# State-space parameters and their powers placed ahead of the modulation's weights, low parts of the first weight columns on VectorE, in a hybrid decoder trunk

## The chip, the cores and the metric

The kernel runs on one core of one Trainium2 chip. A core has five engines with queues of their own: TensorE (PE, with PEld for its weight loads), VectorE (DVE), ScalarE (ACT), GpSimd (POOL) and SyncE (SP), which here only issues DMA transfers. ScalarE's queue issues some transfers too. The metric is the device time of one execution in microseconds; the value for a kernel is the median of its runs.

## The reference

One layer of a trunk, with a prompt of 2048 tokens and 8 short samples of 4 tokens (32 in all), 1024 features, float32. Cut to what matters here:

```python
mod = jnp.dot(jax.nn.silu(c), p['ada_w']) + p['ada_b']
sh1, sc1, g1, sh2, sc2, g2 = jnp.split(mod, 6, axis=-1)
h = x * (1.0 + sc1) + sh1
z = jnp.dot(h, p['in_proj'])            # columns: gate | recurrent | state-space
dt = jnp.exp(log_dt)[:, None]
mag = jnp.exp(dt * ar)
abr, abi = mag * jnp.cos(dt * ai), mag * jnp.sin(dt * ai)
den = ar * ar + ai * ai
nr = abr - 1.0
qr, qi = (nr * ar + abi * ai) / den, (abi * ar - nr * ai) / den
bbr = qr[..., None] * b_re - qi[..., None] * b_im
...
```

A complex diagonal scan with (abr, abi), a gated unit, a real-gated recurrence on the other columns, an output projection, two layer norms and a squared-ReLU MLP follow. The kernel writes the state-space scan in blocks of 8 steps, so that it needs the powers 0 to 8 of abr + i abi.

## The kernel before, in words

Every product is made from a high part (rounded to the fast matmul format) and a low part (the rest): `split` (L77) copies the source to the high part on ScalarE and subtracts it on the engine that it is given. Three matmuls (L373 to L375) make one product.

The opening has this order in the program. ScalarE's queue loads the conditioning vectors c (`crow`), which give `cT`. `ada_early` (L468) loads the weights of modulation section 1, the scale (eight loads of 512 KB on SP's queue), multiplies them with `cT` into `pa`, and between them lets ScalarE's queue issue the 11 loads of small vectors (`vjobs`, L457 to L465: first `ada_b` into `rtA`, then ten into `rtB`). `vec_fin` (L477) transposes them. `ada_fin` (L188) copies `pa` to `adasb`, sums it with `pm` and adds `ada_b` into `mods`; then comes `sc1p`. `load_x` (L385) and `make_h` (L394) bring the first 256 tokens in, transpose them into PSUM (`pt`), scale them into `hf` (VectorE and ScalarE in turns), store `hf` in DRAM (`Hd`) and split it into `a0h` and `a0l`. `load_w` (L197) brings the four column blocks 8 to 11 of in_proj, the state-space columns, into `rwin` and splits them into `hwin` and `lwin`; `WX` (L382) names the engine of each low part: VectorE for the first, GpSimd for the three others. Then `load_x(1)` and `vec_fin("B")`.

After that the generator `s5` (L1457) is made and run to its first yield (L503). This first part loads the state-space parameters with nine small loads on SP's queue (L1513 to L1523; `load`, L1466, puts each behind the last large load), transposes them (`s5pt`), makes dt and mag with two exponentials of some 20 small VectorE operations each (`expf`), sine and cosine on ScalarE, the powers PR and PI (L1555 to L1572), rho, A4r and A4i, then qr, qi and, from the loads of Br and Bi, bbr and bbi (L1580 to L1614), and last copies powers with ScalarE into Q1, Q2, R1, R2 (eight operations of 64x256, L1616 to L1624). Br and Bi stand in the same slots as `rw` and the intermediates of the powers.

`pa0` (L504) brings modulation section 0, the shift, in the same way as section 1. The loop at L514 goes over the eight pieces of 256 tokens: it makes the next piece's h (from piece 2, `BARE`, on with the shift in it), runs `s5` on by one part, multiplies the four column blocks with the piece (`accb`), copies the results (`xb`) and stores them in DRAM (`Ud`). The later parts of `s5` make matrices (Bx, CA, kt) from Q1 to R2, bbr, bbi and the C parameters on VectorE and GpSimd and store them (`BCd`, `Td`). Behind the loop, pairs of state-space groups (`pair`) run between the other columns' products.

The order of each engine's queue is not that of the source. The program is built with `schedule_with_timeline_sim=True` (L1895): at build time, whatever the build holds ready goes to its engine, what stands earlier in the program first, by the build's own picture of durations and landings. On the chip each engine then works its queue in that fixed order, and a head that waits holds all behind it. Tiles with the same tag share a fixed number of buffers.

Of the kernel before, what the change touches and what calls it, by code (L numbers as in the profile page):

```python
# [17 lines left out]
P = 128  # L18
# [17 lines left out]
def trunk(ctx: ExitStack, tc: tile.TileContext, *args):  # L36
# [325 lines left out]
    with lpool("ab") as ab:  # L362
# [19 lines left out]
        WX = V, Q, Q, Q  # L382
# [85 lines left out]
        def ada_early(sec, tile_):  # L468
            pa = ptile([P, 512], "D", f"pa{sec}")
            for k in range(0, KD, 2):  # L470
                ada_mm(pa, k, [ada_load(sec, k + e, tile_(f"ada{sec}_{k + e}")) for e in range(2)])
                for _ in range(2):
                    if vjobs:
                        S.dma_start(*vjobs.pop(0))
            return pa
# [11 lines left out]

        pa1 = ada_early(1, early_tile)
        while vjobs:
# [9 lines left out]
        s5x = ExitStack()  # L499
        s5g = s5(s5x, nc, tc, a, outs, rpool, ptile, ident, (Ud, Yd, BCd, Td), dict(  # L500
            tt=tt, mul=mul, add=add, sub=sub, ts=ts, stt=stt, act=act, f32=f32, split=split, last=last_pair))
# [955 lines left out]
def s5(ctx, nc, tc, a, outs, rpool, ps, ident, scratch, o):  # L1457
# [8 lines left out]
    def load(out, in_):  # L1466
        with tc.issue_after(last[0]):
            SP.dma_start(out, in_)
# [33 lines left out]
    with rpool("s5b") as pool:  # L1502
# [11 lines left out]
        for i, key in enumerate(("s5_a_re", "s5_a_im")):  # L1514
            src = a[key][0]
            load(rw[0:32, i, 0:64], src)
            load(rw[0:32, i, 64:128], src)
            load(rw[32:48, i, :], src.rearrange("(p q) n -> p (q n)", q=2))
        ld2 = one([W, 2], "ld2")
        sl = a["s5_log_dt"]  # L1520
        load(ld2[0:32, 0:1], sl.rearrange("o g -> g o"))
        load(ld2[0:32, 1:2], sl.rearrange("o g -> g o"))
        load(ld2[32:48, :], sl[0].rearrange("(p q) -> p q", q=2))  # L1523
# [55 lines left out]

        nr = small("nr", 32)  # L1580
# [34 lines left out]

        Q1 = one([P, 32, 8], "Q1")  # L1616
        Q2 = one([P, 32, 8], "Q2")
        R1 = one([P, 32, 8], "R1")
        R2 = one([P, 32, 8], "R2")
        for dst, s0, half, sg, src in ((Q1, 7, top, 1, PR), (Q1, 7, bot, 1, PI), (Q2, 7, top, -1, PI),  # L1620
                                       (Q2, 7, bot, 1, PR), (R1, 1, top, 1, PR), (R1, 1, bot, -1, PI),
                                       (R2, 1, top, -1, PI), (R2, 1, bot, -1, PR)):
            x = src[half, 7::-1, GB] if s0 == 7 else src[half, 1:9, GB]
            act(dst[half], x.rearrange("p m g -> p g m"), AF.Copy, scale=float(sg))  # L1624
# [274 lines left out]
```

## Time and profile before

| what | value |
|---|---|
| time, median of 3 runs | 2111.79 us (2110.53 to 2115.14) |
| the profiled execution's own time | 2115.44 us |
| span of its profile | 2113.7 us |
| mean granted TensorE clock | 0.986 |
| busy: PE, DVE, ACT, POOL | 2011.9, 1543.5, 1087.4, 494.0 us |

The profile is of one execution. Busy time is the union of an engine's instructions. A granted clock of 1 means the higher of TensorE's two levels, 2.4 GHz, over the whole stretch; at the lower, 1.2 GHz, it reads 0.5. The DMA share is the mean over 16 DMA engines and can exceed 1 a little, as packets overlap. Small differences between times of one kernel, of a few us, are its spread.

### The profile page before, as it was taken

To read this page: it belongs to the slowest core of one execution; us is meant where nothing else is said; L and a number is where in the kernel's file an instruction comes from. 1 tells how busy PE (TensorE), PEld (TensorE's weight loads), DVE (VectorE), ACT (ScalarE), POOL (GpSimd) and SP (SyncE) were. 2 spreads that over 40 slices of the span, in tenths; PEclk is the share of its full clock that TensorE was granted. 3 is DMA by queue.
4 is the path that set the end of the run, shared out by engine and by line. 5 is a ranking of instruction groups with operands and counts; after the bars stand their busy time and mean duration, and the time that the engine had idled before them with its cause. 6 is when DMAs were issued, how large, how long until landed. Compare 5 with 4: busy or idle time off the path is not lost.

```text
span 2113.7 us, 35579 instructions
## 1 busy us (share of the span) xinstructions
PE 2011.9 (95%) x13055; PEld 1904.1 (90%) x13055; DVE 1543.5 (73%) x2920; ACT 1087.4 (51%) x2077; POOL 494.0 (23%) x327
## 2 busy tenths in 40 slices
PE   7998999889999989999999899999999999999996
PEld 4897888887877879999999899999999999999996
DVE  5678897467887899989898965666747555655587
ACT  3446665445766447554646454635445344444452
POOL 2255333323433233222223300101012001010103
PEclk9999999999999999999999999999999999999998
DMA  9799765543434467968677797878678968686861
GB/s 329 177 263 274 233 197 171 141 137 80 130 94 99 134 244 265 346 248 306 239 278 264 266 323 248 305 268 288 243 260 317 315 229 282 216 270 239 265 218 54
DMA packets 363037, 489.08 MB, mean 231 GB/s; under 512 B 126939, under 2 KB 264575, under 8 KB 362863
## 3 DMA queue, kind: packets, MB, share of 16 engines
q1 hardware_dynamic: 359415, 485.52, 69.6%
q8 instruction: 103, 1.69, 0.3%
q10 hardware_dynamic: 3448, 1.29, 0.2%
q14 instruction: 71, 0.58, 0.1%
HBM read 347.73 MB, written 139.00 MB: 230 GB/s over the span
## 4 chain that ended last, share of the span: by engine, by line
PE 63%; DVE 19%; DMA 6%; issue 5%; ACT 4%; POOL 1%; SPq 1%; ACTq 0%; DVEq 0%; POOLq 0%
PE m1a L1078 19%; PE m2x L1225 13%; PE m1s L1078 8%; PE m2s L1225 6%; PE m2a L1225 3%; DVE xc L62 2%; DVE acc L44 1%; PE accg L373 1%; PE accg L374 1%; PE accg L375 1%; PE op L963 1%; PE pa L185 1%; PE op L964 1%; PE op L962 1%; DVE gi L347 1%
## 5 line engine op out<-in xcount | busy, mean ns | idle before, releaser
L44 POOL TENSOR_TENSOR y<-y,ln_g 128x512 f32<-128x512 f32 (+3 forms) x28 | 36.5, 1320 | 645.8 <-ACT y L65 544.2
L65 ACT ACTIVATE hid<-hid 128x346 f32<-128x346 f32 (+1 forms) x240 | 116.1, 489 | 71.1 <-DVE hid L62 64.3
L65 ACT ACTIVATE ht<-hid 128x692 fp32r<-128x692 f32 (+1 forms) x92 | 72.0, 783 | 127.8 <-PE m2a L1225 38.9
L44 DVE TENSOR_TENSOR lt<-hid,ht 128x692 fp32r<-128x692 f32 (+1 forms) x92 | 85.2, 927 | 40.5 <-ACT ht L65 40.5
L44 DVE TENSOR_TENSOR acc<-m2x,acc 128x346 f32<-128x346 f32 (+1 forms) x168 | 84.1, 511 | 32.0 <-PE m2x L1225 31.7
L44 DVE TENSOR_TENSOR hid<-hid,hid 128x692 f32<-128x692 f32 (+1 forms) x92 | 87.1, 947 | 23.5 <-ACT hid L65 23.3
L1225 PE MATMUL m2x<-ht,hw2s 128*128 128x348 f32 (+1 forms) x352 | 87.7, 322 | 1.8 <-DVE acc L44 1.8
L62 DVE SCALAR_TENSOR_TENSOR hid<-m1s,vecB,u 128x346 f32<-128x346 f32 (+1 forms) x94 | 53.5, 573 | 45.0 <-ACT u L65 35.4
L65 ACT ACTIVATE u<-m1a 128x346 f32<-128x346 f32 (+1 forms) x96 | 43.5, 453 | 70.4 <-PE m1a L1078 63.0
L44 DVE TENSOR_TENSOR lb<-hid,hb 128x692 fp32r<-128x692 f32 (+1 forms) x69 | 69.2, 1004 | 4.7 <-ACT hb L65 4.5
L65 ACT ACTIVATE hb<-hid 128x692 fp32r<-128x692 f32 (+1 forms) x69 | 53.8, 783 | 21.6 <-PE m2a L1225 6.9
L1225 PEld LDWEIGHTS m2x<-ht,hw2s 128*128 128x128 f32 x352 | 61.9, 189 | 2.2 <-ACT hw2s L65 2.1
L65 ACT ACT_TABLE_LOAD x40 | 51.3, 1283 | 15.9 <-DVE hgb L57 6.5
L44 DVE TENSOR_TENSOR acc<-m2s,acc 128x346 f32<-128x346 f32 (+1 forms) x120 | 55.7, 508 | 4.1 <-PE m2s L1225 4.0
L1078 PE MATMUL m1s<-h2t13h,hw1s 128*128 128x348 f32 (+1 forms) x200 | 54.1, 329 | 3.9 <-DVE x L62 3.5
L1225 PE MATMUL m2x<-lt,hw2s 128*128 128x348 f32 (+1 forms) x176 | 56.1, 321 | 0.9 <-DVE lt L44 0.9
L1225 PE MATMUL m2x<-ht,w2s 128*128 128x346 f32 (+1 forms) x216 | 55.9, 321 | 0.0
L1225 PE MATMUL m2s<-ht,hw2s 128*128 128x348 f32 (+1 forms) x208 | 53.2, 331 | 2.6 <-ACT ht L65 2.6
L44 DVE TENSOR_TENSOR u<-m1s,u 128x346 f32<-128x346 f32 (+1 forms) x48 | 24.7, 514 | 42.0 <-PE m1s L1078 27.2
L65 ACT ACTIVATE y<-y,AB,mods 128x128 f32<-128x128 f32 (+2 forms) x96 | 37.5, 472 | 34.5 <-DMA y<-Cd 34.5
L1225 PE MATMUL m2a<-hb,hw2a 128*128 128x348 f32 (+1 forms) x200 | 52.0, 327 | 3.4 <-DVE acc L44 3.4
L1078 PE MATMUL m1a<-h2b1h,hw1a 128*128 128x348 f32 (+1 forms) x208 | 55.1, 323 | 0.0
(854 smaller groups left out, 7982.0 us busy)
## 6 DMA issues: line engine op xcount, KB each, us to landing
W1d<-hw1s SPq DMA_DIRECT2D x53, 512.0 KB
W2d<-hw2s SPq DMA_DIRECT2D x53, 512.0 KB
w1s<-W1d SPq DMA_DIRECT2D x45, 512.0 KB
lw1s<-W1d SPq DMA_DIRECT2D x43, 512.0 KB
hw2s<-W2d SPq DMA_DIRECT2D x41, 512.0 KB
hw1s<-W1d SPq DMA_DIRECT2D x40, 512.0 KB
w2s<-W2d SPq DMA_DIRECT2D x40, 512.0 KB
lw2s<-W2d SPq DMA_DIRECT2D x39, 512.0 KB
```

The source lines that it names most:

```text
L44: return eng.tensor_tensor(out=out, in0=in0, in1=in1, op=op)
L62: return V.scalar_tensor_tensor(out, in0, s, in1, op0, op1)
L65: return S.activation(out, in_, f, **kw).ins
L185: PE.matmul(pa[q:q + 32, :], cT[:, k + e, :], w[:, n * 512:n * 512 + 512], start=(k == 0), stop=(k == KD - 2), tile_position=(0, q))
L347: V.tensor_tensor_scan(gi[:, f, :n], rr[:, f, :n], gi[:, f, :n], 0.0 if pi == 0 else rgs["h"][:, f:f + 1], ALU.mult, ALU.add)
L373: PE.matmul(acc[:, :nt], wh[:, k, :], hh[:, kk, :nt], start=(k == 0), stop=False)
L374: PE.matmul(acc[:, :nt], wh[:, k, :], hl[:, kk, :nt], start=False, stop=False)
L375: PE.matmul(acc[:, :nt], wl[:, k, :], hh[:, kk, :nt], start=False, stop=(k == KD - 1))
L962: PE.matmul(ac[:w, :], yh[:, kk, o:o + w], wh[:, hs], start=(k == 0), stop=False)
L963: PE.matmul(ac[:w, :], yl[:, kk, o:o + w], wh[:, hs], start=False, stop=False)
L1078: PE.matmul(ps, x[:, k, :], h[:, k, o:o + w], start=(on is None and k + i == 0), stop=(k == 3 and i == 2), skip_group_check=on is not None)
L1225: PE.matmul(ps[2 * s_ + jj], x[:, f, js], h[:, f, :], start=(fresh and n + f + e == 0), stop=(n == len(pairs) - 1 and f + e == 3), skip_gr ...
```

## The change

It moves the making of the generator `s5` and its first run ahead of `ada_early(1)`, and gives `s5` one yield more, so that this first run ends behind the powers; the copies into Q1 to R2 now stand ahead of that yield, and the part with qr, qi, Br, Bi, bbr and bbi stays where the whole first part stood. The nine small loads are issued by ScalarE's queue in place of SP's, without the order behind the last large load. The low parts of all four first column blocks are made on VectorE.

```diff
-        WX = V, Q, Q, Q
+        WX = V, V, V, V
...
+        s5x = ExitStack()
+        s5g = s5(s5x, nc, tc, a, outs, rpool, ptile, ident, (Ud, Yd, BCd, Td), dict(
+            tt=tt, mul=mul, add=add, sub=sub, ts=ts, stt=stt, act=act, f32=f32, split=split, last=last_pair))
+        next(s5g)
         pa1 = ada_early(1, early_tile)
         while vjobs:
             S.dma_start(*vjobs.pop(0))
...
         load_x(1)
         vec_fin("B")
-        s5x = ExitStack()
-        s5g = s5(s5x, nc, tc, a, outs, rpool, ptile, ident, (Ud, Yd, BCd, Td), dict(
-            tt=tt, mul=mul, add=add, sub=sub, ts=ts, stt=stt, act=act, f32=f32, split=split, last=last_pair))
 
         next(s5g)
...
-            load(rw[0:32, i, 0:64], src)
-            load(rw[0:32, i, 64:128], src)
-            load(rw[32:48, i, :], src.rearrange("(p q) n -> p (q n)", q=2))
+            S.dma_start(rw[0:32, i, 0:64], src)
+            S.dma_start(rw[0:32, i, 64:128], src)
+            S.dma_start(rw[32:48, i, :], src.rearrange("(p q) n -> p (q n)", q=2))
...
-        load(ld2[0:32, 0:1], sl.rearrange("o g -> g o"))
-        load(ld2[0:32, 1:2], sl.rearrange("o g -> g o"))
-        load(ld2[32:48, :], sl[0].rearrange("(p q) -> p q", q=2))
+        S.dma_start(ld2[0:32, 0:1], sl.rearrange("o g -> g o"))
+        S.dma_start(ld2[0:32, 1:2], sl.rearrange("o g -> g o"))
+        S.dma_start(ld2[32:48, :], sl[0].rearrange("(p q) -> p q", q=2))
...
         V.tensor_copy(A4i[bot], PI[bot, 4, GB])
+
+        Q1 = one([P, 32, 8], "Q1")
+        Q2 = one([P, 32, 8], "Q2")
+        R1 = one([P, 32, 8], "R1")
+        R2 = one([P, 32, 8], "R2")
+        for dst, s0, half, sg, src in ((Q1, 7, top, 1, PR), (Q1, 7, bot, 1, PI), (Q2, 7, top, -1, PI),
+                                       (Q2, 7, bot, 1, PR), (R1, 1, top, 1, PR), (R1, 1, bot, -1, PI),
+                                       (R2, 1, top, -1, PI), (R2, 1, bot, -1, PR)):
+            x = src[half, 7::-1, GB] if s0 == 7 else src[half, 1:9, GB]
+            act(dst[half], x.rearrange("p m g -> p g m"), AF.Copy, scale=float(sg))
+        yield
 
         nr = small("nr", 32)
...
         add(V, bbi, bbi, bt)
-
...
         yield
```

The lines left out ahead of the last yield are the same block of Q1 to R2, taken from there.

## Rows read from the trace of the kernel before

**Rows 1.** The page's parts 1 and 4: busy time, and the chain that ended last.

```profile
PE 2011.9 (95%) x13055; PEld 1904.1 (90%) x13055; DVE 1543.5 (73%) x2920; ACT 1087.4 (51%) x2077; POOL 494.0 (23%) x327
...
PE 63%; DVE 19%; DMA 6%; issue 5%; ACT 4%; POOL 1%; SPq 1%; ACTq 0%; DVEq 0%; POOLq 0%
```

**Rows 2.** Busy time by stretch: PE, PEld, DVE, ACT, POOL, granted clock, DMA share, GB/s.

```profile
21.50:40.00 18.50, 15.37 (x98) 12.91 (x98) 15.36 (x53) 8.06 (x13) 7.76 (x3) 0.91 0.86 296
40.00:64.00 24.00, 24.00 (x165) 17.19 (x165) 19.81 (x125) 8.10 (x17) 2.37 (x1) 1.00 0.65 242
64.00:81.00 17.00, 12.75 (x87) 11.49 (x86) 11.28 (x21) 11.93 (x20) 4.86 (x2) 0.90 0.73 159
81.00:140.00 59.00, 57.82 (x522) 56.00 (x520) 48.09 (x68) 25.82 (x49) 27.27 (x12) 1.00 1.03 262
...
160.00:185.00 25.00, 19.55 (x152) 18.85 (x152) 20.80 (x25) 18.79 (x41) 19.11 (x10) 0.98 1.00 251
```

**Rows 3.** TensorE's waits, 15 to 42 us: total, times, longest.

```profile
PE accb L374 <- DVE a0l L44: 3.1, 3, 1.4
```

**Rows 4.** TensorE's waits, 60 to 82 us.

```profile
PE pt L412 <- ACT hf L65: 3.2, 2, 2.6
```

**Rows 5.** ScalarE's copies into Q1 to R2: first and last of four groups of two.

```profile
L65 ACT ACTIVATE Q<-PR x2: 659/662/664, 66.2 to 66.9; 64x256 f32<-64x256 f32 x2
...
L65 ACT ACTIVATE R<-PI x2: 629/630/632, 72.3 to 72.9; 64x256 f32<-64x256 f32 x2
```

**Rows 6.** VectorE in order of time: start, duration, instruction, idle time before.

```profile
15.76 0.69 DVE L190 COPY adasb<-pa 128x512 f32<-128x512 f32 x1 [6.52 <-PE pa L185]
17.61 0.23 DVE L44 TENSOR_TENSOR mods<-pm,vecA 128x72 f32<-128x72 f32 x1 [1.16 <-PE pm L193]
...
22.10 1.29 DVE L44 TENSOR_TENSOR a0l<-hf,a0h 128x512 fp32r<-128x512 f32 x2
...
25.99 2.53 DVE L44 TENSOR_TENSOR a0l<-hf,a0h 128x512 fp32r<-128x512 f32 x1 [1.08 <-ACT a0h L65]
...
28.72 2.07 DVE L57 TENSOR_SCALAR z<-vecB 128x4 f32<-128x4 f32 x1
...
33.48 0.22 DVE L1524 COPY rw<-ld 48x128 f32<-48x128 f32 x1
```

**Rows 7.** VectorE's groups by form, 20 to 80 us: busy, mean ns, idle before.

```profile
L44 DVE TENSOR_TENSOR a0l<-hf,a0h 128x512 fp32r<-128x512 f32 x4 | 4.5, 1145 | 1.1 <-ACT a0h L65 1.1
...
L44 DVE TENSOR_TENSOR s5ex_p<-s5ex_p,s5ex_r 128x48 f32<-128x48 f32 x12 | 2.5, 205 | 0.0
...
L44 DVE TENSOR_TENSOR lwin<-rwin,hwin 128x1024 fp32r<-128x1024 f32 x1 | 1.2, 1225 | 1.5 <-ACT hwin L65 1.5
```

**Rows 8.** GpSimd in order of time, 22 to 32 us.

```profile
22.99 7.76 POOL L44 TENSOR_TENSOR lwin<-rwin,hwin 128x1024 fp32r<-128x1024 f32 x3 [21.26 <-ACT hwin L65]
```

**Rows 9.** SP's queue in order of time: start and length of issue.

```profile
23.73 1.40 SPq L1468 DMA_DIRECT2D rw<-in_s_a_re_dram  x3
...
29.10 2.00 SPq L1468 DMA_DIRECT2D ld<-in_s_log_dt_dram  x3
...
70.02 2.53 SPq L1468 DMA_DIRECT2D Br<-in_s_b_re_dram  x2
```

**Rows 10.** ScalarE's queue in order of time: its third, eleventh and twelfth issue.

```profile
2.02 0.60 ACTq L474 DMA_DIRECT2D rtA<-in_ada_b_dram  x1
...
13.38 0.28 ACTq L490 DMA_DIRECT2D rtB<-in_mlp_b_dram  x1
13.69 0.44 ACTq L490 DMA_DIRECT2D rtB<-in_ln_g_dram  x1
```

**Rows 11.** The chain that ended last, first 40 us, in order of time.

```profile
2.64 5.85 DMA rtB<-in_mlp_b_dram
8.51 4.64 DMA rtB<-in_rg_bi_dram
```

**Rows 12.** SP's queue's own waits, up to 100 us.

```profile
SPq L160 <- DMA rtB<-in_rg_bi_dram: 0.9, 1, 0.9
```

More of the change, by code (lines that the diff above doesn't have):

```diff
@@ L1614, in s5 @@
         add(V, bbi, bbi, bt)
[L1616 to L1624, printed above, removed]
         yield
```

## The prediction

> **What bounds the kernel now.** The page comes first: TensorE is busy 95% of the span and holds 63% of the chain that ended last [rows 1]. So a change in the first 100 us is worth what it takes out of TensorE's idle time, or out of its slow clock, there. The table by stretch says where that is [rows 2]: from 40 to 64 us TensorE has no gap (24.00 of 24), so nothing that only makes its inputs earlier can pay there. From 64 to 81 us it is busy 12.75 of 17 us at a granted clock of 0.90, and from 21.5 to 40 us 15.37 of 18.5 at 0.91. From 81 to 140 us it is full again (57.82 of 59), while the DMA engines are at 1.03 and VectorE works 48 of 59. From 160 to 185 us, where the first state-space pair starts, it idles 5.4 us with the DMA engines at 1.00.
>
> The waits of TensorE name the causes. From 15 to 42 us it waits 3.1 us for a0l, the low part of the first activations [rows 3]; from 60 to 82 us it waits 3.2 us for ScalarE's hf [rows 4]. In that second stretch ScalarE runs the eight copies into Q1, Q2, R1, R2, from 66.2 to 72.9 us at 0.63 to 0.67 us each [rows 5]: they stand in its queue between the hf copies that empty PSUM for the transposes.
>
> VectorE's order shows the first stretch [rows 6]. One a0l takes 2.53 us and the z of 128x4 behind it 2.07 us. The four a0l take 4.5 us together [rows 7], though the first two took 1.29 us for the pair [rows 6]. GpSimd's three lwin run from 22.99 for 7.76 us [rows 8], and both long instructions end inside that run or with it: VectorE stood still while GpSimd worked.
>
> **The change, part by part.** The 80 VectorE operations from the parameters' copy to A4i (L1524 to L1578), their three transposes, nine small loads and the eight copies get a place in the program ahead of the modulation's weights; all keep their cost. The nine loads leave SP's queue for ScalarE's; SP's queue loses the stretch from 23.73 to 31.1 us, in which they stand with one store [rows 9]. Three lwin go from GpSimd (2.6 us each) to VectorE (1.23 us, the one that is there already [rows 7]).
>
> Start. ScalarE's queue now issues nine more loads ahead of the load of ada_b, which is its third today (2.02 us [rows 10]). As the twelfth it takes the place of the issue at 13.69 us [rows 10]. Two small loads on this queue took 5.85 and 4.64 us from issue to the release of their follower [rows 11], so ada_b lands at 18.3 to 19.5 us, and with its transpose and copy (about 0.6 us) the modulation is added at 18.9 to 20.1 us, not at 17.61 [rows 6]: 1.3 to 2.5 us late. ScalarE's first hwin (1.05 us) stands ahead of a0h and can use that gap, so about 0.6 of it is hidden. I take +1.5, with bounds 0 (the loads land at once) and +4 (issues wait for one another: SP's first load of in_proj already waited for a landing on ScalarE's queue [rows 12], so the queues hold each other up).
> By the lower bound the sum below would give 2104.8. The Trainium skill, "DMA: Bandwidth & Descriptors", section "Queues, rings and completion order", says that each DMA engine takes turns between the queues it has work for, packet by packet; by that rule a small load on ScalarE's queue need not wait out the bulk on SP's, and the start would cost about nothing. The 5.85 us speak against it.
>
> GpSimd's lwin to VectorE. VectorE gets 3 x 1.23 = 3.7 us of work, and loses what it stood still: a0l 4.5 - 4 x 0.65 = 1.9 us and z 2.07 - 0.16 = 1.9 us, together 3.8. In busy time that is even. TensorE's waits for a0l (3.1 us) can go at best; at worst the new lwin and the chain's operations, now first in priority, delay a0l by 3.7 us. Each big operation lets one or two chain operations of 0.2 us in. I take -0.8 between -3.1 and +3.7: the waits are the nearer row, but VectorE has 15.36 of 18.5 us busy in this stretch [rows 2] and receives the chain as well.
>
> The eight copies. Made after the powers, which are then ready some 20 us earlier, they leave ScalarE's queue in the 66 to 73 us stretch and lie where ScalarE is busy 8.10 of 24 us (40 to 64 [rows 2]); 8 x 0.65 = 5.2 us fit there, beside TensorE's full work. If that cover were gone, they would cost up to 5.2 us as now. What goes: the 3.2 us wait for hf. A granted clock of 0.90 over 17 us means 17 x 0.10 x 2 = 3.4 us at 1.2 GHz in place of 2.4, which costs 1.7 us; 1.5 of it goes with the gap before it. Next late is GpSimd's a2l, the low part of the next activations' second half, but it starts when a2h is there, and that is earlier too. Together -4.7, bounds -4.9 and 0.
>
> SP's nine issues. The loads of the shift's weights stand right behind them in SP's queue and can go up to 7 us earlier. TensorE is full from 40 us on, so this alone I cost at 0; it makes the shift earlier, which the term above needs.
>
> Later. The loads of Br and Bi, at 70.0 us today [rows 9], need the slots that the powers free, and the DMA engines are at 0.65 from 40 to 64 us [rows 2]. They and their products come earlier and out of the stretch where the DMA engines are full. TensorE idles 1.2 us from 81 to 140 and 5.4 from 160 to 185 us. I take -1.5 between -6.6 and +2 (the build orders everything behind anew, and a worse order is as possible as a better).
>
> Sum: 1.5 - 0.8 - 4.7 + 0 - 1.5 = -5.5 us. The profiled execution took 2115.4 us (span 2113.7, 1.7 around it), so 2109.9 for it; it stands 3.6 us above the median of 2111.8, and on that median the sum gives 2106.3.
>
> **The rivals.** A, slower: VectorE works in its queue's order, and the copy rw<-ld waits for the last of the nine loads. That is the eleventh issue of ScalarE's queue, 13.38 us today [rows 10], which lands at 18.0 to 19.2 us; transposes and the copy of par make it 20. If the build, which expects the loads earlier, has put this copy and part of the 80 operations ahead of adasb (15.76 us [rows 6]), adasb waits 4.2 us plus 0.2 us for each operation ahead [rows 7]: with half of them 12.2 us. The modulation's first section, the first hf and all that follows wait with it. Against the other terms (-7.0) this gives 2111.8 - 7.0 + 12.2 = 2117.0, from 2109 with none ahead to about 2121 with 60. It decides once adasb runs after about 23 us (15.76 + 7.0). For it: the operations stand first in the program. Against: in the trace of before rw<-ld, at 33.48 us, has no idle time of VectorE ahead of it [rows 6], so the build's picture of such landings was not far off.
> B, no change: the DMA engines bound what follows. They are at 1.03 from 81 to 140 and at 1.00 from 160 to 185 us [rows 2]; the 4.7 us gained before are then waited off ahead of the first pair, where 5.4 us of idle already are. 1.5 - 0.8 = +0.7 is left: 2112.5. Against: at 0.65 and 0.73 in the two stretches ahead, these engines have room for what moves up.
> C, more: the whole state-space preparation (VectorE's Bx and CA) moves up with its parameters, the first pair finds its matrices ready, and most of the later 6.6 us go: some 5 us more, 2101. Against: the pair needs the last columns of the x projection, which the preparation does not make earlier.
>
> **How the numbers follow.** A measurement of this kernel can tell about 0.2%, 4.2 us, from no change: faster is below 2107.6, slower above 2116.0. The forecast has 0.45 (of it 0.30 below 2107.6, 0.12 between, 0.03 above, as its unknown terms reach from -3.1 to +4 around it), A 0.20 (0.16 slower, 0.04 within), B 0.20 (0.17 within, 0.03 slower), C 0.15 (faster). Faster 0.45, same 0.33, slower 0.22. The range of 8 in 10 leaves out C's far half and A's worst: 2099 to 2120; the forecast's own is 2101 to 2112.
>
> **What would show it.** In the trace after: the addition to mods near 19.5 us; a0l all near 0.65 us and no VectorE instruction of 2 us beside GpSimd before 40 us; Q and R copies before 55 us; no wait of TensorE for hf above 1 us between 60 and 80 us, and a granted clock near 1.00 there; Br loaded before 60 us. Wrong would be: adasb after 23 us (A), the front some 5 us earlier at 80 us but not at 200 us (B), or TensorE waiting for lwin or a0l by more than 3 us before 40 us.

## The result, and the profile after

The changed kernel is slower. Its median is 2124.6 us over 6 runs (2121.39 to 2128.51), against 2113.25 for the kernel before over 6 runs beside it (2110.53 to 2115.14): a ratio of 1.0055, with an interval of 1.0041 to 1.0070, or 11.4 us by the medians. The forecast was 2106.3, and its range ended at 2120. The profiled execution of the changed kernel took 2121.39 us (span 2119.6), the lowest of its six, and that of before 2115.44, above its six. So the two profiles show 5.9 us (their spans) of the 11.4, and the rest can't be seen in them. Each profile below is likewise of one execution.

The page's parts 1 and 4, answering to [rows 1]. TensorE has 2.2 us less busy time in a span that is 5.9 us longer:

```profile
PE 2009.7 (95%) x13055; PEld 1901.9 (90%) x13055; DVE 1549.6 (73%) x2923; ACT 1089.2 (51%) x2079; POOL 493.8 (23%) x324
...
PE 57%; DVE 22%; DMA 8%; issue 5%; ACT 5%; POOL 2%; SPq 1%; ACTq 0%; DVEq 0%; POOLq 0%
```

The table by stretch, answering to [rows 2] (PE, PEld, DVE, ACT, POOL, granted clock, DMA share, GB/s), of the changed kernel:

```profile
15.70:21.50 5.80, 4.95 (x39) 3.21 (x29) 2.43 (x11) 0.00 (x0) 0.00 (x0) 1.00 0.53 155
21.50:40.00 18.50, 11.04 (x51) 7.11 (x51) 14.50 (x59) 9.57 (x15) 0.00 (x0) 0.82 1.00 335
40.00:64.00 24.00, 22.68 (x167) 17.95 (x164) 21.41 (x118) 12.28 (x25) 2.45 (x1) 1.00 0.80 257
64.00:81.00 17.00, 16.45 (x141) 16.25 (x140) 14.30 (x27) 8.10 (x15) 3.75 (x2) 1.00 0.74 166
81.00:140.00 59.00, 53.45 (x475) 51.05 (x474) 47.49 (x51) 25.96 (x50) 29.33 (x13) 0.97 0.92 254
...
160.00:185.00 25.00, 20.51 (x161) 19.83 (x160) 13.69 (x12) 16.17 (x31) 18.31 (x14) 1.00 0.99 248
```

and the same table of the kernel before, for the first stretch, which [rows 2] doesn't have:

```profile
15.70:21.50 5.80, 3.05 (x27) 2.61 (x25) 2.54 (x6) 2.38 (x5) 0.00 (x0) 1.00 1.14 306
```

Read down the PE column beside [rows 2]: 1.9 us won from 15.7 to 21.5, 4.3 lost from 21.5 to 40 (at a clock of 0.82 in place of 0.91), 1.3 lost from 40 to 64, 3.7 won from 64 to 81 at a clock of 1.00 in place of 0.90, 4.4 lost from 81 to 140 (at 0.97 in place of 1.00), 1.0 won from 160 to 185.

**The start.** The first product of the column blocks starts 4.3 us late. The kernel before, then the changed kernel (the last two numbers in front of the semicolon are the first and the last start):

```profile
L373 PE MATMUL accb<-a0h,hwin x32: 274/282/420, 21.5 to 45.8; 128*128 128x256 f32 x32
```

```profile
L373 PE MATMUL accb<-a0h,hwin x32: 277/282/583, 25.8 to 53.9; 128*128 128x256 f32 x32
```

In the first row of the table the DMA share has fallen from 1.14 to 0.53. SP's queue's own waits say why, answering to [rows 12]:

```profile
SPq L160 <- DMA rtA<-in_ada_b_dram: 5.6, 1, 5.6
```

The first load of in_proj stands in SP's queue until ada_b, a small load on ScalarE's queue with which it shares no data, has landed. In order of time (start, length of issue), ScalarE's issue of ada_b and SP's four of in_proj, answering to [rows 10]:

```profile
13.63 0.43 ACTq L474 DMA_DIRECT2D rtA<-in_ada_b_dram  x1
```

```profile
17.67 6.66 SPq L160 DMA_DIRECT2D rwin<-in_in_proj_dram  x4
```

In the records of the trace the transfers of both queues use eight semaphores in turn, and each waits until the one that had its semaphore before has landed. In the build's order ada_b is the eighth before the first load of in_proj. Before, that was rg_bi, and the wait 0.9 us [rows 12].

**The second half of hf.** The chain that ended last, 24 to 37 us (start, us, what), answering to [rows 11] and to VectorE's order [rows 6]:

```profile
24.16 1.06 ACT hwin L65
25.21 0.52 ACT a0h L65
...
26.68 0.37 ACT hf L65
...
27.07 8.73 DMA Hd<-hf
...
35.83 0.49 DVE hf L57
...
36.92 0.30 PE vpsB L480
```

The second half of hf waits for the buffer of the first half, whose store to `Hd` takes 8.73 us to land (3.90 us in the same chain before). Two of the shift's 512 KB loads are now issued ahead of it, at 25.47 and 25.95 us, and the store only at 27.07; that these loads make the store slow is argued, and no run separates it.

**VectorE**, answering to [rows 6] and [rows 7]:

```profile
17.07 0.69 DVE L190 COPY adasb<-pa 128x512 f32<-128x512 f32 x1 [7.57 <-PE pa L185]
17.68 0.21 DVE L1525 COPY rw<-ld 48x128 f32<-48x128 f32 x1
...
19.04 0.23 DVE L44 TENSOR_TENSOR mods<-pm,vecA 128x72 f32<-128x72 f32 x1 [0.79 <-PE pm L193]
...
35.83 0.48 DVE L57 TENSOR_SCALAR hf<-pt,sc1p 128x256 f32<-128x256 f32 x1 [1.97 <-DMA Hd<-hf]
```

```profile
L44 DVE TENSOR_TENSOR lwin<-rwin,hwin 128x1024 fp32r<-128x1024 f32 x4 | 4.9, 1220 | 2.7 <-ACT hwin L65 2.7
...
L44 DVE TENSOR_TENSOR a0l<-hf,a0h 128x512 fp32r<-128x512 f32 x4 | 2.7, 682 | 0.0
```

adasb runs ahead of the parameters' copy, mods is 1.43 us late, and a0l takes 0.68 us each, as forecast. TensorE's waits from 15 to 42 us have moved, though, from a0l (3.1 us before [rows 3]) to what makes it possible. The kernel before, then the changed kernel:

```profile
PE accb L373 <- ACT a0h L65: 2.0, 1, 2.0
```

```profile
PE accb L373 <- ACT a0h L65: 5.1, 1, 5.1
PE vpsB L480 <- ACT hf L65: 1.8, 1, 1.8
...
PE accb L374 <- DVE a0l L44: 0.5, 1, 0.5
```

a0h stands in ScalarE's queue behind hwin, which waits for the late load of in_proj (24.16 us in the chain above).

**64 to 81 us.** ScalarE's copies, answering to [rows 5], run from 57.2 to 63.2 us:

```profile
57.22 1.31 ACT L65 ACTIVATE Q<-PR 64x256 f32<-64x256 f32 x2 [2.34 <-DVE PR L44]
...
61.91 1.34 ACT L65 ACTIVATE R<-PI 64x256 f32<-64x256 f32 x2
```

The wait for hf from 60 to 82 us [rows 4] is 1.3 us, in two. **81 to 97 us** gives this back. The matrices come earlier too, and VectorE stands still beside GpSimd (VectorE, then GpSimd, in order of time):

```profile
81.24 2.05 DVE L57 TENSOR_SCALAR Cs<-CT 64x512 f32<-64x512 f32 x1
83.33 2.32 DVE L57 TENSOR_SCALAR hxb<-hxb,accb 128x256 f32<-128x256 f32 x1
85.57 0.34 DVE L57 TENSOR_SCALAR lxb<-lxb,accb 128x256 f32<-128x256 f32 x1
```

```profile
79.69 3.32 POOL L44 TENSOR_TENSOR tm<-Q,bbi 128x1024 f32<-128x1024 f32 x1 [8.11 <-PE s5ph L1664]
82.97 2.53 POOL L44 TENSOR_TENSOR a3l<-hf,a3h 128x1024 fp32r<-128x1024 f32 x1
```

hxb takes 2.32 us here and lxb, an operation of the same size right behind it, 0.34; TensorE waits 2.8 us for the xb that ScalarE can only then make. From 97 to 140 us it waits 1.7 us more for kt (VectorE) and 0.8 for hf.

**From 0 to 470 us, and from there to 760.** The same view in two long stretches, the kernel before and then the changed kernel:

```profile
0.00:470.00 470.00, 427.05 (x3304) 375.00 (x3305) 340.81 (x763) 246.98 (x560) 164.43 (x121) 0.98 0.73 213
470.00:760.00 290.00, 269.00 (x1515) 224.80 (x1514) 232.59 (x501) 176.69 (x270) 97.83 (x50) 0.98 0.41 114
```

```profile
0.00:470.00 470.00, 428.82 (x3316) 375.43 (x3317) 342.69 (x767) 249.60 (x562) 160.03 (x118) 0.99 0.73 214
470.00:760.00 290.00, 262.02 (x1483) 218.77 (x1482) 229.49 (x493) 175.91 (x268) 92.91 (x49) 0.96 0.41 111
```

At 470 us TensorE of the changed kernel is no longer behind: it has been busy 1.8 us more, at a clock of 0.99 and not 0.98. The late opening has been waited off in between: the first state-space pair starts 8.5 us late (its first product `pv` at 180.1 us, 171.6 before), the gated unit 1.4 us late (`pg` at 391.2, 389.8 before). The loss that the profile shows comes from 470 to 760 us, where TensorE is busy 7.0 us less at a clock of 0.96 and not 0.98.

### The profile page after: what moved, and what is told of

Same layout as the page of the kernel before. It is cut to its first block, busy times and chain, and to the rows that moved or that the text cites. A ratio compares the mean times of both kernels' runs of the same rounds, so it can differ in the third digit from the quotient of the medians.

```text
span 2119.6 us, 35579 instructions
## 1 busy us (share of the span) xinstructions
PE 2009.7 (95%) x13055; PEld 1901.9 (90%) x13055; DVE 1549.6 (73%) x2923; ACT 1089.2 (51%) x2079; POOL 493.8 (23%) x324
## 4 chain that ended last, share of the span: by engine, by line
PE 57%; DVE 22%; DMA 8%; issue 5%; ACT 5%; POOL 2%; SPq 1%; ACTq 0%; DVEq 0%; POOLq 0%
PE m1a L1079 19%; PE m2x L1226 13%; PE m1s L1079 7%; PE m2s L1226 6%; PE m2a L1226 3%; DVE xc L62 1%; DVE acc L44 1%; PE accg L373 1%; PE accg L375 1%; PE accg L374 1%; DVE lspare L44 1%; DVE hw2s L44 1%; DVE lt L44 1%; DVE E L62 1%; DVE gi L347 1%
## 5 line engine op out<-in xcount | busy, mean ns | idle before, releaser
L963 PE MATMUL op<-hwo,ybh 128*128 128x512 f32 x128 | 51.9, 407 | 6.5 <-ACT ybh L65 6.5
```

Of the source, the lines that this page charges most:

```text
L963: PE.matmul(ac[:w, :], yh[:, kk, o:o + w], wh[:, hs], start=(k == 0), stop=False)
```

## The experiments

Every time below is a median with the ratio to runs of the kernel before beside it, whose medians lay between 2113.2 and 2114.5 us. What the expectations call the order is that of the built programs' queues. Where they count runs of equal instructions, TensorE's sequence was compared with repeats of one product taken as one: from the gated unit's first product to the end, 7 of 100 stand elsewhere in the changed kernel than in the kernel before. Set side by side in the same way, TensorE's products in the traces show four orders from there on: that of the kernel before (1, 7, 11, 13, 17), that of the changed kernel or within 1 of 100 of it (2, 3, 4, 5, 8, 10, 12), one with some 2 of 100 elsewhere than before (9, 14, 16), and a third one (6, 15).

**1. The low parts alone.**

```diff
-        WX = V, Q, Q, Q
+        WX = V, V, V, V
```

> The kernel before with the change's last part alone: all four low parts of the first weight columns on VectorE. Theory (the loss comes from the nine small loads in front): this part is innocent; GpSimd's three low parts go, a0l takes about 0.65 us each, SP's first load of in_proj still goes near 13.2 us, the first product still starts near 21.5 us, and the time is 2108 to 2116 us, within 4 us of the kernel before. Rival (VectorE has too much to do in the first 40 us): a0l comes later than 31.2 us, TensorE waits over 3 us more before 40 us, and the time is 2117 us or more.

2110.75 us, 0.9994 (0.9984 to 1.0004). The low parts are innocent, and worth nothing that can be measured. TensorE's wait for a0l up to 82 us goes from 3.1 to 1.0 us, and its wait for hf there from 3.2 to 4.3.

**2. The loads in front, alone.** The generator is made and run to a new yield behind the loads; all else stays.

```diff
+        next(s5g)
         pa1 = ada_early(1, early_tile)
...
-            load(rw[0:32, i, 0:64], src)
+            S.dma_start(rw[0:32, i, 0:64], src)
...
         load(ld2[32:48, :], sl[0].rearrange("(p q) -> p q", q=2))
+        S.dma_start(ld2[32:48, :], sl[0].rearrange("(p q) -> p q", q=2))
+        yield
```

> The kernel before with one thing of the change alone: the nine small loads stand in front of ada_b on ScalarE's queue, while the 80 operations on the parameters, the eight copies and GpSimd's low parts stay where they were. Theory (SP's first load of in_proj has to wait for the landing of ada_b, and the section 0 weights that move up in SP's queue then hold up the store of the first half): SP waits some 5.6 us for ada_b as in the changed kernel, the first product starts near 25.5 us, and the time is 2118 to 2126 us. Rival (the operations in front of VectorE's queue do the harm): SP waits under 2 us, the first product starts at 22 to 23.5 us, and the time stays at 2110 to 2116 us.

2123.33 us, 1.0050 (1.0035 to 1.0065): nearly the whole loss. SP's waits and the first product:

```profile
SPq L160 <- DMA rtA<-in_ada_b_dram: 5.4, 1, 5.4
```

```profile
L373 PE MATMUL accb<-a0h,hwin x32: 278/304/582, 25.6 to 54.2; 128*128 128x256 f32 x32
```

The operations ahead of the modulation are not needed for the loss; the nine loads are enough.

**3. The change with its first part behind the small vectors.**

```diff
-        next(s5g)
         pa1 = ada_early(1, early_tile)
         while vjobs:
             S.dma_start(*vjobs.pop(0))
+        next(s5g)
```

> The changed kernel with its new first part put behind the eleven loads of small vectors, so that the nine loads come after ada_b and the others on ScalarE's queue; operations, copies and low parts as changed. Theory: SP's first load of in_proj goes near 13.2 us again, mods is added near 17.6 us, the first product starts at 21.5 to 22.5 us, and the time falls by 4 to 12 us against the changed kernel, to 2112 to 2120 us; what is left over the kernel before is the store behind the section 0 weights. Rival (the operations in front do the harm): the first product starts after 24 us and the time stays within 3 us of the changed kernel.

2120.74 us, 1.0035 (1.0022 to 1.0048). mods is back at 17.23 us, but SP's first load of in_proj still goes at 17.27, after 5.2 us of waiting, now for ln_g, and the first product starts at 24.8. The theory's picture of the start was too narrow: any small load that is the eighth before holds it. Its time lies 3.9 us below the changed kernel's, between what the theory and what the rival said.

**4. Own buffers for rtA and rtB**, in the changed kernel.

```diff
-            rt = ab.tile([P, 4, 288], F32, tag="hf", name="rt" + nm, bufs=2)[:, 0, 0:P]
+            rt = ab.tile([P, 384], F32, tag="stg", name="rt" + nm, bufs=4)[:, 0:P]
```

> The changed kernel with the two small-vector tiles rtA and rtB in buffers of the output staging (free at that time) and no longer in the two buffers of hf. Theory (second loss: the second half of the first hf waits for a buffer that the store of the first half holds for 8.7 us behind the section 0 weights): both halves of hf are written by 25 us, TensorE's idle time between 30 and 36 us goes, the first product still starts near 25.5 us, and the time falls by 4 to 8 us, to 2116 to 2121 us. Rival (TensorE lacks weights there and not hf): TensorE idles as long from 25 to 40 us, now for lwin or hwin, and the time stays within 3 us of the changed kernel.

2124.2 us, 1.0050 (1.0033 to 1.0066). The second half of hf no longer waits for the store (all of hf by 27.4 us, not 36.9), TensorE is busy 13.15 us from 21.5 to 40 instead of 11.04, and the time is the same. So 2 us of TensorE's time in the opening were worth nothing that shows at the end. (The profiled execution took 2132.57 us, over 8 more than the other three.)

**5 and 6. The loads on GpSimd's queue**, in the changed kernel, and with the edit of 4 as well.

```diff
-            S.dma_start(rw[0:32, i, 0:64], src)
+            Q.dma_start(rw[0:32, i, 0:64], src)
...
```

> The changed kernel with the nine small loads, at the same place in front, issued by GpSimd's queue in place of ScalarE's. Theory (the harm comes from landings that SP's next load has to wait for, since a transfer takes the slot of the eighth one before it among SP's and ScalarE's, and not from the bytes nor from the operations in front): SP's wait ahead of its first load of in_proj falls from 5.6 us to under 1.5 us, that load goes near 13.2 us, the first product starts at 21 to 22.5 us and not at 25.8, and the time falls by 4 to 12 us against the changed kernel, to 2112 to 2120 us. Rival A (the operations in front, or the small transfers themselves, do the harm): the first product stays after 24 us and the time within 3 us of the changed kernel. Rival B (GpSimd's loads land late): the parameters' copy waits, and VectorE with it, past 20 us.

> The kernel with the nine loads on GpSimd's queue, and rtA and rtB in buffers of the output staging as well. Theory: both losses are gone; the first product starts at 21 to 22.5 us, hf's second half is written by 24 us, the stretch from 21.5 to 40 us has TensorE busy over 15.4 us at a clock over 0.91, and the time is below the kernel before: 2102 to 2111 us. Rival (what is gained in the first 80 us is waited off behind, where the DMA engines are full): busy as said until 80 us, but the time within 4 us of the kernel before.

2136.21 us, 1.0103 (1.0084 to 1.0122), and 2137.81 us, 1.0117 (1.0102 to 1.0132). The first product came back as the theory said, that of run 5 as early as before:

```profile
L373 PE MATMUL accb<-a0h,hwin x32: 277/282/582, 21.5 to 54.9; 128*128 128x256 f32 x32
```

SP's first load of in_proj went at 13.37 us. So the wait does come from ScalarE's landings. Rival B did not come: the parameters' copy ran at 18.35 us, behind the addition to mods (17.97). But only the first product is mended, not the opening: the last start in the line is 54.9 us, against 45.8 in the kernel before, from 21.5 to 40 us TensorE is busy 14.20 us at a clock of 0.54 (15.37 at 0.91 before [rows 2]), and the first pair starts at 190.4 us, 18.8 late. In 6, where both losses of the theory were to be gone, that stretch has 14.22 us at 0.72, not over 15.4 at over 0.91. And the time rose by twice the loss that was to be explained. So a first product on time does not bring the time back, and the order of what follows came into question; that the opening costs nothing is not shown by these two.

**7. The copies alone**, ahead of qr and qi, in the old place.

```diff
+        Q1 = one([P, 32, 8], "Q1")
...
+            act(dst[half], x.rearrange("p m g -> p g m"), AF.Copy, scale=float(sg))
+        yield
+
         nr = small("nr", 32)
```

> The kernel before with one thing of the change alone: the eight copies into Q1, Q2, R1, R2 stand right behind the powers, ahead of qr, qi, Br and Bi; place, loads and low parts as before. The forecast's term for the copies: they leave the stretch from 66 to 73 us, TensorE's wait for hf between 60 and 80 us falls from 3.2 us to under 1 us, and the time falls by 2 to 5 us, to 2108 to 2111 us. Rival (given back: TensorE's next stretch, 81 to 185 us, is held by the DMA engines and the state-space chain anyway): the wait for hf goes, TensorE idles as much more between 81 and 205 us, and the time stays within 2 us of the kernel before.

2113.01 us, 1.0003 (0.9994 to 1.0013). TensorE's wait for hf up to 82 us stays at 3.2 us: without powers that are ready earlier the copies go no earlier.

**8. The edit of 4 in the kernel before.**

> The kernel before with rtA and rtB in buffers of the output staging and no longer in hf's two. Theory (the second half of the first hf waits for the store of the first half: 3.90 us in the chain of the kernel before, 8.7 us in the changed one): hf's second half is written by 22 us and not at 24.0, TensorE's wait for a0l and a0h before 42 us falls from 5.1 us by 2 to 4 us, and the time falls by 1 to 4 us, to 2109 to 2112 us. Rival (the weights' high and low parts set the pace there): TensorE waits as long, for hwin or lwin, and the time stays within 1 us.

2124.75 us, 1.0055 (1.0037 to 1.0073): as slow as the changed kernel, with a first product at 21.8 us. The theory missed in its parts too: TensorE's wait for a0l and a0h before 42 us is 5.5 us, not less than 5.1. The two tiles changed the build's order everywhere behind, and nothing of the change is in this kernel. What the new order looks like is seen in TensorE's waits from 470 to 765 us. The kernel before:

```profile
PE pg L311 <- DVE gy L62: 4.4, 7, 1.2
...
PE nt L995 <- DVE x L59: 3.6, 4, 2.4
...
PE op L962 <- ACT ybh L65: 2.9, 1, 2.9
```

and the changed kernel:

```profile
PE op L963 <- ACT ybh L65: 6.5, 1, 6.5
PE nt L996 <- DVE x L59: 6.4, 1, 6.4
PE nt L996 <- DVE rs_1t L632: 3.3, 2, 2.5
```

Run 8 has these waits too (7.3, 6.4 and 3.0 us), and so have 2, 3, 10 and 12.

**9 to 12. Order against start.** 9 is 3 and 4 together. 10 has the low parts, the copies and the first part one step earlier, on SP's queue:

```diff
         wxb = [load_w(8 + m, WX[m], wpa) for m in range(4)]
+        next(s5g)
         load_x(1)
         vec_fin("B")
```

11 is 1 and 7 together, and 12 changes one number far behind the opening:

```diff
-        PAIR_U = [2.25 * i for i in range(17)] + [99]
+        PAIR_U = [2.0 * i for i in range(17)] + [99]
```

> The changed kernel with both edits of the earlier runs: its first part behind the eleven loads of small vectors, and rtA and rtB in buffers of the output staging. In the order that the build gives TensorE from the gated unit's first product on, it is nearly the kernel before again (2 of 100 runs of equal instructions stand elsewhere, against 7 of 100 for the changed kernel), while its opening has the nine loads, the operations and the copies of the change. Theory O (most of the loss comes from the order that the build gives to what follows, hundreds of microseconds behind the edit): the first product still starts after 24 us, as SP waits near 5 us for a landing, and yet the time is 2111 to 2117 us. Theory S (the late start itself is the loss): the time is 2118 to 2123 us.

> The kernel before with the low parts on VectorE, the copies behind the powers, and the state-space first part one step earlier: behind the weights of in_proj and ahead of the second piece's x. The nine loads stay on SP's queue, behind the fourth load of in_proj. From the other columns' products on, its order is that of the changed kernel and not that of the kernel before. Theory O: SP's first load of in_proj goes near 13 us and the first product starts near 21.5 us, and yet the time is 2118 to 2125 us. Theory S: with the start mended the time is 2108 to 2116 us.

> The change without its loads and its place: low parts on VectorE and copies behind the powers, in the kernel before; the order behind the first 100 us stays that of the kernel before. By the forecast's two terms (-0.8 and -4.7) 2108 us; by the two single runs, which gave ratios of 0.9994 and 1.0003, no change: 2110 to 2115 us. I expect the latter: the copies wait for an operation chain that the edit doesn't make earlier.

> The kernel before with one number changed far behind the opening: a pair of state-space groups every 2.0 column products and not every 2.25. The first 160 us keep their order instruction for instruction; from the gated unit's first product on, the order is that of the changed kernel (1 of 100 runs of equal instructions stand elsewhere). Theory O: 2117 to 2124 us, with a first product at 21.5 us. Theory S: within 3 us of the kernel before, 2110 to 2117 us.

9: 2132.82 us (2119.41 to 2134.62), 1.0080 (1.0055 to 1.0105), with the first product at 25.8. Neither theory has this. An order close to that of the kernel before is no protection. Its profile is of the execution of 2119.41 us, at least 11 us faster than its other four, so the loss can't be seen in it.
10: 2119.13 us (2109.52 to 2126.65), 1.0028 (1.0013 to 1.0042), with the first product at 21.6.
11: 2111.91 us, 0.9999 (0.9986 to 1.0011).
12: 2121.88 us, 1.0040 (1.0024 to 1.0056), with an opening as before and the first product at 21.3. Its waits from 470 to 765 us are those of the changed kernel:

```profile
PE nt L995 <- DVE x L59: 6.7, 1, 6.7
PE op L962 <- ACT ybh L65: 6.3, 1, 6.3
...
PE nt L995 <- DVE rs_1t L631: 2.8, 2, 2.0
```

So kernels with an order like that of the changed kernel are 5.9 and 8.5 us slower without a late start (10, 12; by the intervals 2.7 to 11.8).

**13 to 17. A late start with the order kept, and the reverse.** Five or nine loads more, ahead of ada_b, into rows of rtA that nobody reads; 16 and 17 put them on GpSimd's queue (`Q`). 15 is 12 with 2.2.

```diff
+        spare_rows, _, _ = vec["A"]
+        for i in range(5):
+            S.dma_start(spare_rows[64 + 4 * i:68 + 4 * i, :], bass.AP(tensor=a["rg_br"].tensor,
+                        offset=a["rg_br"].offset, ap=[[P, 4], [1, P]]))
         def ada_early(sec, tile_):
```

> The kernel before with five small loads more in front of ada_b on ScalarE's queue, into rows that nobody reads; nothing else changes, and the order of all that follows the opening is that of the kernel before, instruction for instruction. Theory sum (loss = late start + new order behind): SP waits 2 to 5 us for a small load's landing ahead of in_proj, the first product starts 1.5 to 4 us late, and the time rises by about as much, 1 to 5 us: 2115 to 2119 us. Theory order alone: the late start is waited off behind, and the time stays within 1 us of the kernel before.

> The same with nine such loads, as many as the change puts in front. Behind the opening the order is still nearly that of the kernel before (none of its products stands elsewhere until the gated unit, 2 of 100 runs of equal instructions from there on). Theory sum: the first product starts near 25.5 us as in the changed kernel, and the time rises by 4 to 6.5 us, to 2117.5 to 2120.5 us, about half of the changed kernel's loss; the other half needs the new order. Theory start alone: the whole 10 to 12 us, 2123 to 2126 us. Theory order alone: under 2 us, below 2116 us.

> The kernel before with a pair every 2.2 column products and not every 2.25: the opening stays instruction for instruction, and from the gated unit's first product on the order is a third one (8 of 100 runs of equal instructions elsewhere than before, 7 of 100 elsewhere than in the changed kernel). If any other order than that of the kernel before costs time: slower by 4 to 10 us, 2118 to 2124 us. If it is the changed kernel's order that is bad: within 3 us of the kernel before.

> The nine spare loads of the run before, issued by GpSimd's queue; the order behind the opening is as there (none of TensorE's products elsewhere than in the kernel before until the gated unit, 2 of 100 from there on). If the 6.8 us of the nine spare loads come from the late first product, that is from SP's wait for a landing on ScalarE's queue: SP's first load of in_proj goes near 13 us, the first product starts at 21 to 22 us, and the time is within 2.5 us of the kernel before. If they come from the 2 of 100 that stand elsewhere: the first product is on time, and yet the time rises by 4 us or more.

> The five spare loads on GpSimd's queue; all of TensorE's products stand as in the kernel before. If small loads on GpSimd's queue cost nothing by themselves: within 2 us of the kernel before. If they cost time by themselves (which could explain why the changed kernel with its loads on GpSimd took 22 us more than the kernel before): over 5 us more.

| run | first product | order behind | median | ratio (interval) |
|---|---|---|---|---|
| 13, five, ScalarE | 22.6 us | as before | 2117.40 us | 1.0016 (1.0007 to 1.0025) |
| 17, five, GpSimd | 21.9 us | as before | 2114.66 us | 1.0007 (0.9998 to 1.0016) |
| 14, nine, ScalarE | 26.4 us | 2 of 100 elsewhere | 2119.95 us | 1.0032 (1.0021 to 1.0043) |
| 16, nine, GpSimd | 21.2 us | 2 of 100 elsewhere | 2120.51 us | 1.0030 (1.0018 to 1.0043) |
| 15, pairs at 2.2 | 21.0 us | a third one | 2126.43 us | 1.0065 (1.0048 to 1.0082) |

After 14 alone, 6.8 us would have been booked on the late start, as its expectation had it; 16 shows that this is wrong. The same loads without the late start (5.2 us earlier) cost the same, to within some 4 us by the two intervals. In 16 TensorE's products that stand elsewhere are all behind 780 us; 14 has such ones there too, and another order of its products in the opening, up to 67 us. 13 went by the theory of the sum: with the order kept and a first product 1.1 us late it is 3.4 us slower (1.5 to 5.3). 15 is 13.7 us slower, more than the 4 to 10 expected if any other order costs time; so it is not the changed kernel's order alone that costs.

16 and 17 side by side show the place. A stretch of 16:

```profile
900.00:950.00 50.00, 48.13 (x302) 47.87 (x301) 45.67 (x61) 29.43 (x57) 12.55 (x9) 0.99 0.62 224
```

of 17, with 50.00 from 900 to 950 as in the kernel before and in 1, 7, 11 and 13 (4, 5, 6 and 15 have 50.00 as well; their losses lie elsewhere):

```profile
900.00:950.00 50.00, 50.00 (x317) 50.00 (x316) 43.34 (x64) 29.84 (x57) 13.70 (x9) 1.00 0.65 240
```

and of the changed kernel:

```profile
900.00:950.00 50.00, 48.13 (x303) 47.87 (x302) 45.65 (x62) 29.17 (x57) 12.40 (x9) 1.00 0.60 223
```

From the first to the last m1a product (the MLP) it is 1304.0 us in 16, 1294.9 in 17 and 1297.3 in the kernel before:

```profile
L1081 PE MATMUL m1a<-h2b1h,hw1a x208: 315/321/493, 731.2 to 2035.2; 128*128 128x348 f32 x52, 128*128 128x346 f32 x52
```

```profile
L1081 PE MATMUL m1a<-h2b1h,hw1a x208: 315/321/425, 732.7 to 2027.6; 128*128 128x348 f32 x52, 128*128 128x346 f32 x52
```

```profile
L1078 PE MATMUL m1a<-h2b1h,hw1a x208: 315/321/408, 732.7 to 2030.0; 128*128 128x348 f32 x52, 128*128 128x346 f32 x52
```

Up to 731 us run 16 is not behind at all, and it loses everything in the MLP, where not a line was edited. In 14 the MLP takes 1303.3 us as well, and it starts at 731.5: the first product's 4.9 us are waited off by then. The changed kernel's own loss lies mostly elsewhere: its MLP takes 1299.6 us, and starts 3.6 us late (736.3), behind the stretch from 470 to 760 us. 17 also answers its own question: five small loads on GpSimd's queue cost nothing that can be measured (0.07%).

## Why the prediction was wrong

**The step that failed** is the term "Later": "-1.5 (-6.6..+2) (the build orders everything behind anew, and a worse order is as possible as a better)". The mechanism was named, and its size and sign were guessed: no row stands behind the +2. Measured: the four kernels that keep the order and the start lie between 0.9994 and 1.0007 (1, 7, 11, 17). All those with an order changed anywhere behind, whatever the edit, are slower: by 6.3 us where the opening and all until 700 us are as before (16: 2114.49 x 0.0030), by 8.5 and 13.7 where only the pair spacing changed (12 and 15), by 5.9 with a first product on time and the changed order (10). No new order was better. The order of the kernel before is kept by some edits and lost by others, and not by their size: one number (12, 15) or two tiles' buffers (8) lose it. By 10, 12, 15 and 16 the term lay between +6 and +14.

**Start**, +1.5 (0 to +4). The modulation came 1.43 us late, inside the 1.3 to 2.5 worked out, but by luck: ada_b had landed by 17.7 us, earlier than the 18.3 to 19.5 forecast, and mods waited for TensorE's pm, behind adasb, which itself came 1.31 us late behind pa. Nor was the modulation the last to come: the first product was 4.3 us late, because SP's load of in_proj waited 5.6 us for ada_b. The text used SP's 0.9 us [rows 12] to widen the bound, and did not ask which load stands behind ada_b in that turn. At the end this costs little: 14 and 16, with 5.2 us between their first products, differ by 0.0002, within their intervals (some 4 us either way), and 13 against 17 gives 0.0009 (some 2 us), with intervals that overlap; 13 alone is 3.4 us above the kernel before. The Trainium skill ("DMA: Bandwidth & Descriptors", section "Anatomy of one DMA — SWDGE (gpsimd) path") says that DMA engines don't wait on semaphores, and that the issuing sequencer does. The trace agrees, on SP's queue: it stood for 5.6 us, up to 17.67, while the DMA engines worked on other transfers at a share of 0.75 (1.05 before in the same stretch). The section of the Trainium skill that the prediction cited, by which queues take turns, is neither shown nor refuted here: the wait lay ahead of any turn.

**SP's nine issues, 0.** Wrong in its reason. "TensorE is full from 40 us on" looked only at what comes earlier; the shift's weights, 5.7 us earlier (25.47 for 31.14), went ahead of the store of hf, which had 3.90 us in the chain before and 8.73 after. TensorE lost 4.3 us of busy time from 21.5 to 40; the rows put 1.8 us of waiting to this, and the larger wait, 5.1 us for a0h (2.0 before), to the late in_proj. Run 4 took this wait away and gained nothing at the end.

**Low parts, -0.8.** Right in its parts (1.22 us each, a0l 0.68, no standstill beside GpSimd before 40 us), and measured alone at -1.3 us, with an interval of -3.4 to +0.8.

**The copies, -4.7.** Right in place: 3.7 us more busy time from 64 to 81 and a clock of 1.00, at which 3.4 us at the lower level cost 1.7. They ran at 57 to 63 us, not before 55: the last powers PR that the first of them waits for were ready 9 us earlier than before (57.2 for 66.2), not the 20 assumed. Without the new place they gain nothing (7, 11). But the next late thing was not a2l; it was VectorE held beside GpSimd from 81 to 86 us (2.8 us of TensorE's waits), then kt, and 4.4 us went from 81 to 140.

**The rivals.** A had the sign and not the mechanism: adasb ran at 17.07 us, far from the 23 that A needs. B, that the gain is waited off later, happened in part, through VectorE and GpSimd and not through the DMA engines, whose share from 81 to 140 fell to 0.92; but the front was never the 5 us ahead at 80 us that B begins with. That a reordering far behind could be the whole loss was not among the rivals.

**What stays open.** Of the 11.4 us some 6 to 8.5 are what kernels with an order like this lose in 10 and 12, and 0 to 5 the start (13, 14, 16). The rest is not told apart, nor is which instruction out of place costs the most.

The granted clock goes along with the loss. Its mean over the six executions of the changed kernel is 0.981, over the 85 of the kernel before beside runs 1 to 17 it is 0.985; 12 and 15 have 0.980, 5 has 0.978, 16 has 0.983, 1 and 11 have 0.985. An estimate from these means: 0.004 x 2120 = some 8 us of the 11.4, if TensorE had work all that time. Whether the new order's waits bring the lower clock, as the stretch from 470 to 760 us suggests, or it comes on its own, no run separates.

Why the nine loads on GpSimd's queue cost 22 us (5) is not settled, but the traces show that the order behind is not the whole of it. 2 and 5 have the same order of TensorE's products from the gated unit on, product for product, and their ratios are 1.0050 and 1.0103; at the gated unit's first product 5 is 12.8 us behind the kernel before (402.6 us), and 2 is 0.4 behind (390.2). So an opening can cost time as well: the 8.5 us by which the first pair was late in the changed kernel were all but waited off by the gated unit, and of the 18.8 in 5 12.8 were left. 9 has the order of 16 from there on, product for product, with another opening, and costs 0.0050 more; its profile can't show why.

## What to carry to other kernels

Where a build orders queues by its own picture of time, an edit in the first 40 us can be an edit of everything behind it: compare the orders first, and give the reordering a term and a range of its own, taken from edits that change nothing but the order. A kernel that was kept because it measured well may owe part of that to its order; that is an argument, which no run here tests. And to learn what a late start costs, make it late without touching the order, and then reorder without making it late; one of the two alone would have told the wrong story here. The first product alone does not say how late an opening is: in 5 it is on time, and the first pair is 18.8 us late.

## What the runs showed that was not expected

- A small load on one queue can hold a 512 KB load on another with which it shares nothing: 5.6 us for ada_b, 5.2 for ln_g (3), 4.7 for conv_b (13). On GpSimd's queue such loads held SP by 0.4 us (16).
- TensorE absorbed a first product 5 us late (14): the gated unit starts 1.0 us late (390.8 us), the MLP 1.2 us early (731.5), and at the end 14 and 16 differ by 0.0002, with intervals of some 4 us.
- A VectorE operation on 128x256 took 2.32 us while GpSimd worked on 128x1024, and 0.34 us without.
- Some orders spread more than others: run 10 from 2109.52 to 2126.65 us, and the kernel before, beside it, from 2108.22 to 2116.39.
